# New places for attention blocks, state-space copies and state-space outputs between the projection units of a decoder block

## The chip, the core and the metric

The kernel runs on one core of a Trainium2 chip. Its engines are TensorE (PE, matrix multiplication; PEld is its loading of weights), VectorE (DVE), ScalarE (ACT) and GpSimd (POOL); SyncE (SP) issues the DMAs that bring weights and inputs from memory. Each engine works through its own queue in order and waits there for results of the others. The metric is the device time of one execution in microseconds (us), less is better.

## The reference

One decoder layer on 512 tokens of width 1024, in float32. A first RMSNorm is followed by one combined input projection; from it three branches are computed, gated, summed, projected and added to the input; a gated convolutional feed-forward layer and a last RMSNorm follow. Cut to what the change touches:

```python
proj = h @ w_in
qa, ka, va, qd, kd, vd, u, g = jnp.split(proj, cuts, axis=-1)
ya, _ = banded_attention(qa, ka, va, 127, attn_sinks)     # branch A: 8 heads, blocks of 128 queries
yb = dilated_attention(qd, kd, vd)                        # branch B: three dilations
yc = s5_mixer(u, ...)                                     # branch C: diagonal complex state space, 32 groups
gates = sigmoid(g)
merged = gates[0]*(ya @ w_branch_a) + gates[1]*(yb @ w_branch_b) + gates[2]*(yc @ w_branch_c)
x = x + merged @ w_out
x = x + conv_ffn(rmsnorm(x), w_up, conv_w, conv_b, w_down)
out = rmsnorm(x)
```

## The kernel before

Each large matrix product keeps float32 accuracy by splitting both operands into a high and a low part (`whi` and `wlo` for weights) and multiplying three times. A weight chunk comes by DMA into `raw`; ACT copies the high part out of it (L66, `whi<-raw`, 128x1024, two per chunk) and DVE subtracts to get the low part (L92, `wlo`).

The work is a list of **units**. A unit is one output tile of a large product: for a projection 24 matmuls of 128x512 (lines 171 to 173), after which ACT copies the result out of PSUM (`pj`, or `th` with a tanh for a gate). Unit 0 ends the projection of u; units 1 to 4 are the queries of branch A (qA), 5 its keys, 6 its values (vA), 7 to 14 the gates of A, 15 and 16 the keys of B, 17 and 18 queries of B, 19 and 20 the values of B (vB), 21 to 24 further queries of B, and from 25 on come the branch projections, gates, the output projection and the feed-forward. Two units share a chunk.

Small work is put between the units by hand. `before(u, f, ...)` has the functions f emitted ahead of unit u's matmuls. `run` emits, for each unit, the splits (whi, wlo) of the next chunk that are due, then the functions of `before`, then the unit; for units in the table `AUX_FIRST` the functions come ahead of those splits. So these tables set the order of every engine's queue. The pieces placed this way:

- `attn_a(i)`, block i of branch A, a generator of steps that `st_(A[i])` takes one at a time. Step 1: scores of half the heads (PE, `sc<-pj`) and their row maxima (DVE, `smA<-sc,maskA`). Step 2: the other half, then `esA` and eight exponentials (ACT), then the scaling by 1/l (DVE, L269). Then transposes (`pt<-ident,smA`) with copies `pTA` on ACT, the product with the values (`o<-pTA,VA`) and its copy `ya` (ACT, and `ya` again on DVE for the low part).
- branch C, in four parts j of 8 groups. `ssm_bd(j)` spreads a table and copies u into `us` (DVE, L624); `ssm_inj(j)` transposes (`pt<-ident,bd`), copies `inj` out (ACT) and fills `tz`; `ssm_cpow` computes the powers `Vw` on POOL with the scratch tiles `vt`; `ssm_ob(j)` copies from Vw into `ob` (ACT, four copies); `ssm_m1(j)` multiplies and scans in two steps (`z`, `X`); `ssm_m2(j)` is the output product (`o<-us,tz`, `o<-X,ob`), whose result goes in four copies of 32x512 to `yS`, two on ACT and two on DVE in turn (lines 724 to 729).
- `to_nat`, four transposes of the projected values (`pt<-ident,pj`, L737) and a copy on ACT (`VA`, `VB`).

Most intermediate tiles are taken by `slot()` from one pool `sl` of 46 equal buffers, in rotation: a new tile takes the buffer of the one taken 46 earlier, and its first writer waits until the last user of that one is done. PSUM has four kinds of banks (`mm`, `sc`, `pt`, `o`), two buffers each, in rotation as well.

Of the kernel before, what the change touches and what calls it, by code (L numbers as in the profile page):

```python
# [14 lines left out]
AX = mybir.AxisListType  # L15

NWARM = 32
AUX_FIRST = (7, 8, 10, 11, 14, 15, 18, 19, 20, 33, 35)
T = 512
DM = 1024  # L20
KD = DM // 128
# [10 lines left out]
def hybrid_block(  # L32
# [7 lines left out]
    V, S, G, PE, SY = nc.vector, nc.scalar, nc.gpsimd, nc.tensor, nc.sync  # L40
# [23 lines left out]
    def copy_act(o, i, scale=None):  # L64
        if scale is None:
            S.activation(o, i, AF.Copy)  # L66
        else:
            S.activation(o, i, AF.Copy, scale=scale)
# [128 lines left out]
    def before(u, *fns):  # L197
        plan.setdefault(u, []).extend(fns)

    def run(first, live):  # L200
# [31 lines left out]
        for u, (c, fn) in enumerate(units):  # L232
# [5 lines left out]
            later.clear()  # L238
            if u in AUX_FIRST:
                for f in fs:  # L240
# [372 lines left out]
    def expand(dst, src, j, scale=None):  # L613

        for g in range(2):
            p = slice(64 * g, 64 * g + 64)
            copy_act(dst[p, :, :, g, :], src[p].rearrange("p k (t j) h -> p t k j h", j=4)[:, :, :, j, :], scale=scale)

    def ssm_bd(j):
        for i in range(2):  # L620
            expand(BDs[j % 2][i], W[0][:, i], j)
        US[j] = slot([128, 4, 128], name="us")
        for tau in range(4):
            V.tensor_copy(US[j][32 * tau:32 * tau + 32],  # L624
                          uT[0][32 * j:32 * j + 32].rearrange("p t (c a) -> p t c a", a=4)[:, :, :, tau])

    def ssm_inj(j):
        bd = BDs[j % 2]
        INJ[j] = [slot([128, 4, 128], name="inj") for _ in range(2)]
        for i in range(2):  # L630
            pb = bank("pt")
            for t in range(4):
                PE.transpose(pb[:, t * 128:(t + 1) * 128],
                             bd[i][:, t].rearrange("p k g h -> p (k g h)"), ident)
            copy_act(INJ[j][i][:, :, :], pb[:, :].rearrange("p (t c) -> p t c", t=4))
        pk = bank("o", (128, 4, 32))
        for t in range(4):
            for i in range(2):
                PE.matmul(pk[:, t, :], bd[i][:, t].rearrange("p k g h -> p (k g h)"),
                          V0b[i][:, 4 * t + j].rearrange("p g h -> p (g h)"), start=(i == 0), stop=(i == 1))  # L640
        tz = TZ[j]
        for ti in range(4):
            for to in range(ti + 1, 4):
                b = 3 - (to - ti)
                copy_act(tz[32 * ti:32 * ti + 32, :, to, :], pk[32 * b:32 * b + 32, :, :])
        for ti in range(4):
            tt(tz[32 * ti:32 * ti + 32, :, ti, :], pk[96:128, :, :],
               DI[0][96:128].rearrange("p (t j) c -> p t j c", j=4)[:, :, j, :], ADD)

    def ssm_ob(j):  # L650
        for i in range(2):
            expand(OB[j][i], Vw[0][:, i], j, None if i == 0 else -1.0)
# [5 lines left out]
    def ssm_e(j):  # L658
        def v(tab):
            return tab.rearrange("p (t j) b -> p t j b", j=4)[:, :, j, :]  # L660

        b = [v(t)[:, :, None, :].to_broadcast([128, 4, 8, 16]) for t in eb]
        a = [v(t)[:, :, :, None].to_broadcast([128, 4, 8, 16]) for t in ea]
        E = [slot([128, 4, 8, 16], name="E") for _ in range(2)]
        t0 = slot([128, 4, 8, 16], name="et")
        tt(E[0], b[0], a[0], MUL, G)
        tt(t0, b[1], a[1], MUL, G)
        tt(E[0], E[0], t0, SUB, G)
        tt(E[1], b[0], a[1], MUL, G)
        tt(t0, b[1], a[0], MUL, G)  # L670
        tt(E[1], E[1], t0, ADD, G)
        Es[j] = [e[:, :, :, :].rearrange("p t a b -> p (t a b)") for e in E]
        A4s[j] = slot([128, 4, 128], name="a4")
        V.tensor_copy(A4s[j], mag4.rearrange("p (t j) -> p t j", j=4)[:, :, j:j + 1].to_broadcast([128, 4, 128]))
        V.memset(A4s[j][:, :, 0:1], 0.0)

    def ssm_m1(j):
        Er, Ei = Es.pop(j)
        s = []
        inj = INJ.pop(j)  # L680
        for i in range(2):
            pb = bank("sc", (128, 4, 128))
            for t in range(4):
                PE.matmul(pb[:, t, :], inj[i][:, t, :], US[j][:, t, :], start=True, stop=True)
            s.append(pb[:, :, :].rearrange("p t c -> p (t c)"))
        a, b, zr, zi = (slot([128, 512], name="z")[:, :] for _ in range(4))
        tt(zr, s[0], Er, MUL)
        tt(a, s[1], Ei, MUL)
        tt(zi, s[1], Er, MUL)
        tt(b, s[0], Ei, MUL)  # L690
        tt(zr, zr, a, ADD, G)
        tt(zi, zi, b, SUB, G)
        a4 = A4s.pop(j)[:, :, :].rearrange("p t c -> p (t c)")
        V.tensor_tensor_scan(a, a4, zr, 0.0, op0=MUL, op1=ADD)
        V.tensor_tensor_scan(b, a4, zi, 0.0, op0=MUL, op1=ADD)
        yield
        X = [slot([128, 4, 128], name="X") for _ in range(2)]
        x3 = slot([128, 512], name="xt")[:, :]

        def sh(v):  # L700
            return v.rearrange("p (t c) -> p t c", c=128)[:, :, 0:127]

        for i in range(2):
            G.memset(X[i][:, :, 0:1], 0.0)
        tt(zr, a, Er, MUL)
        tt(x3, b, Ei, MUL)
        tt(X[0][:, :, 1:128], sh(zr), sh(x3), SUB, G)
        tt(zi, a, Ei, MUL)
        tt(b, b, Er, MUL)
        tt(X[1][:, :, 1:128], sh(zi), sh(b), ADD, G)  # L710
        Xs[j] = X
        yield

    def ssm_m2(j):
        if not yS:
            yS.append(y8([128, 4, T], name="yS"))
        X, tz, us, ob = Xs.pop(j), TZ.pop(j), US.pop(j), OB.pop(j)
        py = bank("o", (128, 4, 128))
        for t in range(4):
            PE.matmul(py[:, t, :], tz[:, t].rearrange("p a b -> p (a b)"), us[:, t, :], start=True, stop=False)  # L720
            for i in range(2):
                PE.matmul(py[:, t, :], ob[i][:, t].rearrange("p k g h -> p (k g h)"), X[i][:, t, :],  # L722
                          start=False, stop=(i == 1))
        for tau in range(4):
            o = yS[0][32 * j:32 * j + 32].rearrange("p t (c a) -> p t c a", a=4)[:, :, :, tau]
            if tau % 2:
                V.tensor_copy(o, py[32 * tau:32 * tau + 32])
            else:
                copy_act(o, py[32 * tau:32 * tau + 32])


    def to_nat(src, name, strided=False):

        pb = bank("pt")
        v = src[:, :].rearrange("p (i r) -> p r i", r=4) if strided else src[:, :].rearrange("p (b i) -> p b i", b=4)
        for b in range(4):
            PE.transpose(pb[:, b * 128:(b + 1) * 128], v[:, b, :], ident)  # L737
        o = slot([128, 4, 128], name=name)
        copy_act(o, pb[:, :].rearrange("p (b c) -> p b c", b=4))
        return o  # L740

    proj = {}
# [10 lines left out]
    VA = []  # L753
# [89 lines left out]
    VB = {}  # L843
# [501 lines left out]
    def st_(g):  # L1345
        return lambda: next(g)

    CP = ssm_cpow()
    A = [attn_a(i) for i in range(4)]
    B = [attn_b(i) for i in range(2)]  # L1350
    M = [ssm_m1(j) for j in range(4)]
    before(0, lambda: pump(99), ssm_b, lambda: pump(6), ssm_phase)
# [2 lines left out]
    before(3, lambda: ssm_bd(0))  # L1355
    before(4, lambda: ssm_inj(0), lambda: ssm_bd(1), lambda: ssm_e(0), st_(CP))
    before(5, lambda: ssm_inj(1), lambda: ssm_bd(2))
    before(6, lambda: ssm_inj(2), lambda: ssm_bd(3), st_(CP))
    M = [ssm_m1(j) for j in range(4)]
    before(7, lambda: ssm_inj(3), st_(A[0]))  # L1360
    before(8, lambda: VA.append(to_nat(proj["vA"], "VA")), lambda: ssm_ob(0), st_(A[0]))
    before(9, st_(M[0]), lambda: ssm_ob(1))
    before(10, st_(A[0]), st_(M[0]), lambda: ssm_ob(2), st_(A[1]))
    before(11, st_(A[0]), lambda: ssm_ob(3), st_(A[1]))
    before(12, lambda: ssm_m2(0), lambda: ssm_e(1))
    before(13, st_(A[1]), st_(M[1]))
    before(14, st_(A[1]), st_(M[1]), st_(A[2]))
    before(15, st_(A[1]), lambda: ssm_m2(1), st_(A[2]))
    before(16, lambda: ssm_e(2))
    before(17, st_(A[2]), st_(M[2]))  # L1370
    before(18, st_(A[2]), st_(M[2]), st_(A[3]))
    before(19, st_(A[2]), lambda: ssm_m2(2), st_(A[3]))
    before(20, lambda: VB.setdefault(0, [to_nat(proj["vB", 0], "VB0")]), lambda: ssm_e(3))
    before(21, st_(A[3]), st_(M[3]), lambda: VB[0].append(to_nat(proj["vB", 0], "VB1", True)))
    before(22, st_(A[3]), st_(M[3]), lambda: VB.setdefault(1, [to_nat(proj["vB", 1], "VB0")]))
    before(23, st_(A[3]), lambda: VB[1].append(to_nat(proj["vB", 1], "VB1", True)))
# [44 lines left out]
```

## Time and profile before

| | |
|---|---|
| time, median of 3 runs | 839.66 us (839.02 to 839.73) |
| the profiled execution | 839.8 us, its span 838.0 us |
| PE busy | 815.6 us (97%) |
| DVE, ACT, POOL busy | 474.1 us (57%), 354.5 us (42%), 164.5 us (20%) |
| mean granted clock of TensorE | 0.991 of 2.4 GHz |

The span runs from the first to the last recorded instruction, and 1.8 us of the execution lie around it. PE is busy nearly throughout, so the questions are where it isn't, and where its clock is low; the places are found in the list of what PE waited for, and then on the timelines of the engines around them.

### The profile page before, as it was taken

The numbers are of one execution on the slowest core, as the hardware profiler recorded it, in microseconds if no ns is written. First come the engines' busy times: TensorE is split into PE (matmuls) and PEld (weight loads), VectorE is DVE, ScalarE is ACT, GpSimd is POOL, SyncE is SP. The second block draws the span as 40 slices with busy tenths as digits, with TensorE's granted clock in tenths as the row PEclk, the third lists the DMA queues.
The fourth block names the chain that finished last, engine by engine and source line by source line (L and its number), as shares of the span: only waits on it lengthen the run. The fifth ranks groups of instructions, "written<-read, shape, count | busy, mean of one in ns | idle before, by whom it ended". The sixth has DMA issues, their size and how long they took to land.

```text
span 838.0 us, 10521 instructions
## 1 busy us (share of the span) xinstructions
PE 815.6 (97%) x4085; PEld 675.9 (81%) x4085; DVE 474.1 (57%) x921; ACT 354.5 (42%) x665; POOL 164.5 (20%) x217
## 2 busy tenths in 40 slices
PE   8999899997999999999999999999999999999996
PEld 7978768775787888888878998888888888888885
DVE  7998387484645637263655456555655555422313
ACT  6446455434435555352444344444444443313212
POOL 6199652441200100023520000000000000002002
PEclk9999989998999999999999999999999999999999
DMA  9332031121322113232261313333233323412402
GB/s 241 102 104 97 1 100 52 51 79 46 78 68 90 52 51 102 79 101 72 101 236 65 101 52 101 101 101 100 101 101 100 102 76 101 153 61 89 151 0 101
DMA packets 68277, 76.60 MB, mean 91 GB/s; under 512 B 8160, under 2 KB 55556, under 8 KB 68228
## 3 DMA queue, kind: packets, MB, share of 16 engines
q1 hardware_dynamic: 67972, 75.89, 28.2%
q8 instruction: 32, 0.52, 0.3%
q0 software_dynamic: 256, 0.05, 0.1%
q14 instruction: 17, 0.14, 0.1%
HBM read 73.81 MB, written 2.12 MB: 91 GB/s over the span
## 4 chain that ended last, share of the span: by engine, by line
PE 80%; POOL 8%; DVE 6%; ACT 2%; issue 2%; DMA 2%; SPq 0%; POOLq 0%; DVEq 0%; ACTq 0%
PE up L171 10%; PE up L172 10%; PE up L173 10%; PE mm L171 9%; PE mm L173 9%; PE mm L172 9%; PE acc L178 6%; PE acc L179 6%; PE acc L177 6%; POOL esc L279 1%; POOL vt L279 1%; POOL t L279 1%; PE sc L898 1%; DMA raw<-in_w_in_dram 1%; PE o L722 1%
## 5 line engine op out<-in xcount | busy, mean ns | idle before, releaser
L92 DVE TENSOR_TENSOR wlo<-raw,whi 128x1024 fp32r<-128x1024 f32 (+1 forms) x126 | 150.0, 1200 | 136.0 <-ACT whi L66 135.8
L66 ACT ACTIVATE whi<-raw 128x1024 fp32r<-128x1024 f32 (+1 forms) x126 | 127.3, 1023 | 58.3 <-PE acc L179 56.2
L171 PE MATMUL up<-hTh,whi 128*128 128x512 f32 (+1 forms) x384 | 142.7, 372 | 0.0
L172 PE MATMUL up<-hTl,whi 128*128 128x512 f32 (+1 forms) x384 | 142.6, 371 | 0.0
L173 PE MATMUL up<-hTh,wlo 128*128 128x512 f32 (+1 forms) x384 | 142.6, 371 | 0.0
L171 PE MATMUL mm<-hTh,whi 128*128 128x512 f32 (+1 forms) x336 | 133.9, 399 | 2.7 <-ACT whi L66 2.7
L173 PE MATMUL mm<-hTh,wlo 128*128 128x512 f32 (+1 forms) x336 | 131.3, 391 | 1.6 <-DVE wlo L92 1.6
L172 PE MATMUL mm<-hTl,whi 128*128 128x512 f32 (+1 forms) x336 | 130.9, 390 | 0.0
L275 DVE SCALAR_TENSOR_TENSOR cc<-up,cpar,cc 128x511 f32<-128x511 f32 x88 | 65.9, 749 | 97.3 <-ACT cc L1110 95.7
L173 PEld LDWEIGHTS up<-hTh,wlo 128*128 128x128 f32 x384 | 72.4, 188 | 12.6
L171 PEld LDWEIGHTS up<-hTh,whi 128*128 128x128 f32 x384 | 72.4, 188 | 12.5
L172 PEld LDWEIGHTS up<-hTl,whi 128*128 128x128 f32 x384 | 72.4, 188 | 12.4
L171 PEld LDWEIGHTS mm<-hTh,whi 128*128 128x128 f32 x336 | 64.3, 191 | 17.9 <-ACT whi L66 3.1
L173 PEld LDWEIGHTS mm<-hTh,wlo 128*128 128x128 f32 x336 | 64.2, 191 | 15.2 <-DVE wlo L92 2.0
L172 PEld LDWEIGHTS mm<-hTl,whi 128*128 128x128 f32 x336 | 64.2, 191 | 11.9
L177 PE MATMUL acc<-whi,gh 128*128 128x512 f32 x172 | 66.9, 389 | 0.0
L178 PE MATMUL acc<-wlo,gh 128*128 128x512 f32 x172 | 66.9, 389 | 0.0
L179 PE MATMUL acc<-whi,gl 128*128 128x512 f32 x172 | 66.9, 389 | 0.0
L279 POOL TENSOR_TENSOR x<-x,gfin 128x512 f32<-128x512 f32 x4 | 5.2, 1289 | 296.8 <-ACT acc L1049 296.8
L1110 ACT ACTIVATE cc<-up,cpar 128x512 f32<-128x512 f32 x44 | 34.3, 779 | 61.2 <-PE up L173 60.4
L992 ACT ACTIVATE th<-mm 128x512 f32<-128x512 f32 x24 | 14.3, 594 | 75.2 <-PE mm L173 75.2
L66 ACT ACTIVATE gh<-cc 128x512 fp32r<-128x512 f32 x22 | 13.9, 632 | 59.4 <-DVE cc L279 59.4
(298 smaller groups left out, 1266.1 us busy)
## 6 DMA issues: line engine op xcount, KB each, us to landing
raw<-in_w_up_dram SPq DMA_DIRECT2D x22, 1024.0 KB, 5.1
raw<-in_w_in_dram SPq DMA_DIRECT2D x18, 1024.0 KB, 5.1
raw<-in_w_down_dram SPq DMA_DIRECT2D x10, 1024.0 KB, 5.0
x<-in_x_dram SPq DMA_DIRECT2D x8, 512.0 KB, 6.6
raw<-in_w_in_dram SPq DMA_DIRECT2D x8, 512.0 KB, 5.3
raw<-in_w_out_dram SPq DMA_DIRECT2D x4, 1024.0 KB, 5.1
raw<-in_w_branch_a_dram SPq DMA_DIRECT2D x4, 512.0 KB, 6.0
raw<-in_w_branch_c_dram SPq DMA_DIRECT2D x2, 1024.0 KB, 5.0
```

Of the source, the lines that this page charges most:

```text
L66: S.activation(o, i, AF.Copy)
L92: (lo_eng or V).tensor_tensor(view(lo), r, view(hi).bitcast(F32), op=ALU.subtract)
L171: PE.matmul(ps, wh, xh, start=first, stop=False)
L172: PE.matmul(ps, wh, xl, start=False, stop=False)
L173: PE.matmul(ps, wl, xh, start=False, stop=last)
L177: PE.matmul(ps, xh, wh, start=first, stop=False)
L178: PE.matmul(ps, xh, wl, start=False, stop=False)
L179: PE.matmul(ps, xl, wh, start=False, stop=last)
L275: emit(lambda: V.scalar_tensor_tensor(o, a, s, b, op0=op0, op1=op1))
L279: emit(lambda: (eng or V).tensor_tensor(o, a, b, op=op))
L992: S.activation(t, ps, AF.Tanh, scale=0.5)
L1110: S.activation(dst, ps, AF.Identity, bias=cpar[:, 3, f:f + 1], scale=cpar[:, 2, f:f + 1])
```

## The change

It moves steps among the units, takes five units (8, 10, 14, 18, 20) out of `AUX_FIRST`, and puts all four copies of each state-space output on ACT. A second, equal line that made the generators M anew is dropped; no step had been taken from the first ones.

```diff
-AUX_FIRST = (7, 8, 10, 11, 14, 15, 18, 19, 20, 33, 35)
+AUX_FIRST = (7, 11, 15, 19, 33, 35)
...
-            if tau % 2:
-                V.tensor_copy(o, py[32 * tau:32 * tau + 32])
-            else:
-                copy_act(o, py[32 * tau:32 * tau + 32])
+            copy_act(o, py[32 * tau:32 * tau + 32])
...
-    before(6, lambda: ssm_inj(2), lambda: ssm_bd(3), st_(CP))
-    before(7, lambda: ssm_inj(3), st_(A[0]))
-    before(8, lambda: VA.append(to_nat(proj["vA"], "VA")), lambda: ssm_ob(0), st_(A[0]))
-    before(9, st_(M[0]), lambda: ssm_ob(1))
-    before(10, st_(A[0]), st_(M[0]), lambda: ssm_ob(2), st_(A[1]))
-    before(11, st_(A[0]), lambda: ssm_ob(3), st_(A[1]))
+    before(6, lambda: ssm_inj(2), lambda: ssm_bd(3), st_(CP), st_(A[0]))
+    before(7, st_(A[0]), lambda: ssm_inj(3))
+    before(8, lambda: VA.append(to_nat(proj["vA"], "VA")), lambda: ssm_ob(0), lambda: ssm_ob(1))
+    before(9, st_(A[0]), st_(M[0]), lambda: ssm_ob(2))
+    before(10, lambda: ssm_ob(3), st_(A[0]), st_(M[0]), st_(A[1]))
+    before(11, st_(A[1]))
...
-    before(15, st_(A[1]), lambda: ssm_m2(1), st_(A[2]))
-    before(16, lambda: ssm_e(2))
+    before(15, st_(A[1]), st_(A[2]))
+    before(16, lambda: ssm_m2(1), lambda: ssm_e(2))
...
-    before(19, st_(A[2]), lambda: ssm_m2(2), st_(A[3]))
-    before(20, lambda: VB.setdefault(0, [to_nat(proj["vB", 0], "VB0")]), lambda: ssm_e(3))
+    before(19, st_(A[2]), st_(A[3]))
+    before(20, lambda: ssm_m2(2), lambda: VB.setdefault(0, [to_nat(proj["vB", 0], "VB0")]), lambda: ssm_e(3))
```

Three places in the engines' queues show what that moves.

The first is ACT from the copy of unit 6 on, with the engines whose semaphores each instruction waits for (the 49 belongs to the semaphore's name). Before, the two `inj` copies of the last state-space part come first and the exponentials of block 0 after the first `ob`:

```order
L66 ACTIVATE pj<-mm 128x512 [waits PE_49,Pool_49]
L66 ACTIVATE inj<-pt 128x512 [waits PE_49] x2
L66 ACTIVATE tz<-o 32x4x32 [waits PE_49]
L66 ACTIVATE tz<-o 32x4x32 x5
L66 ACTIVATE whi<-raw 128x1024 [waits DMAHW4_49,DVE_49]
L992 ACTIVATE th<-mm 128x512 [waits PE_49,Pool_49]
L66 ACTIVATE VA<-pt 128x512 [waits PE_49,Pool_49]
L66 ACTIVATE ob<-Vw 64x16x16 x2
L68 ACTIVATE ob<-Vw 64x16x16 x2
L780 ACTIVATE esA_1233<-esA_1233 128x8 [waits DVE_49]
L782 ACTIVATE smA,lA_1232<-smA,nmA_1231 128x128 x2
```

And now:

```order
L66 ACTIVATE pj<-mm 128x512 [waits PE_49]
L777 ACTIVATE esA_1173<-esA_1173 128x8 [waits DVE_49]
L779 ACTIVATE smA,lA_1172<-smA,nmA_1171 128x128 [waits Pool_49]
L779 ACTIVATE smA,lA_1172<-smA,nmA_1171 128x128
L779 ACTIVATE smA,lA_1172<-smA,nmA_1171 128x128 [waits Pool_49]
L779 ACTIVATE smA,lA_1172<-smA,nmA_1171 128x128 x3
L779 ACTIVATE smA,lA_1172<-smA,nmA_1171 128x128 [waits Pool_49]
L779 ACTIVATE smA,lA_1172<-smA,nmA_1171 128x128
L66 ACTIVATE inj<-pt 128x512 [waits PE_49,Pool_49] x2
L66 ACTIVATE tz<-o 32x4x32 [waits PE_49]
L66 ACTIVATE tz<-o 32x4x32 x5
L66 ACTIVATE whi<-raw 128x1024 [waits DMAHW4_49]
```

The exponentials of block 0 stand ahead of the last `inj` copies, and through the rotation of the buffers it is now these two copies that wait for POOL: they take the buffers of the two scratch tiles `vt`, which `th` and `VA` took before. Both splits (`whi`) of the next chunk stand behind them.

The second is DVE at units 8 to 11, from the scaling of block 0 to the first row maximum of block 1. Before:

```order
L269 TENSOR_SCALAR smA<-smA,lA_1232 128x128 x8
L92 TENSOR_TENSOR wlo<-raw,whi 128x1024 x2
L279 TENSOR_TENSOR z<-sc,E 128x512 x4
L694 SCALAR_TENSOR_TENSOR z<-a_992,z 128x512
L695 SCALAR_TENSOR_TENSOR z<-a_992,z 128x512
L279 TENSOR_TENSOR z<-z,E 128x512
L279 TENSOR_TENSOR xt<-z,E 128x512
L279 TENSOR_TENSOR z<-z,E 128x512 x2
```

And now:

```order
L269 TENSOR_SCALAR smA<-smA,lA_1172 128x128 x8
L279 TENSOR_TENSOR tz<-o,DI 32x4x32 x4
L92 TENSOR_TENSOR wlo<-raw,whi 128x1024 x3
L279 TENSOR_TENSOR z<-sc,E 128x512 x4
L694 SCALAR_TENSOR_TENSOR z<-a_992,z 128x512
L695 SCALAR_TENSOR_TENSOR z<-a_992,z 128x512
L92 TENSOR_TENSOR wlo<-raw,whi 128x1024
L279 TENSOR_TENSOR ya_1363<-o,ya_1362 128x4x128
L279 TENSOR_TENSOR z<-z,E 128x512
L279 TENSOR_TENSOR xt<-z,E 128x512
L279 TENSOR_TENSOR z<-z,E 128x512 x2
```

The maxima of block 1 have one more split (`wlo`) and the second part of `ya` ahead of them, behind the scans.

The third is ACT at units 18 to 20, from the `ya` copy of block 2 to the copies around the first `VB`. Before:

```order
L66 ACTIVATE ya_1411<-o 128x4x128
L66 ACTIVATE yS<-o 32x512 x2
L780 ACTIVATE esA_1999<-esA_1999 128x8
L782 ACTIVATE smA,lA_1998<-smA,nmA_1997 128x256 x8
L66 ACTIVATE whi<-raw 128x1024
L66 ACTIVATE pj<-mm 128x512
L66 ACTIVATE VB_2135<-pt 128x512
L66 ACTIVATE whi<-raw 128x1024
```

And now:

```order
L66 ACTIVATE ya_1362<-o 128x4x128
L777 ACTIVATE esA_2005<-esA_2005 128x8
L779 ACTIVATE smA,lA_2004<-smA,nmA_2003 128x256 x8
L66 ACTIVATE whi<-raw 128x1024
L66 ACTIVATE pj<-mm 128x512
L66 ACTIVATE whi<-raw 128x1024
L66 ACTIVATE yS<-o 32x512 x4
L66 ACTIVATE VB_2142<-pt 128x512
L66 ACTIVATE pj<-mm 128x512
```

The `yS` copies of state-space part 2 stood ahead of the exponentials of block 3, and now stand behind them and behind the copy `pj` of unit 19, four in a row.

## Rows read from the trace of the kernel before

**Rows 1.** Busy time of each engine over the span, first part of the page.

```profile
PE 815.6 (97%) x4085; PEld 675.9 (81%) x4085; DVE 474.1 (57%) x921; ACT 354.5 (42%) x665; POOL 164.5 (20%) x217
```

**Rows 2.** What PE waited for: total us, times, longest us.

```profile
PE pt L737 <- ACT pj L66: 5.4, 1, 5.4
PE mm L171 <- ACT whi L66: 2.7, 1, 2.7
PE mm L173 <- DVE wlo L92: 1.6, 1, 1.6
```

**Rows 3.** Stretches: length, busy us (count) per engine, granted clock, DMA, GB/s.

```profile
107.10:112.80 5.70, 5.70 (x18) 4.51 (x18) 5.43 (x6) 1.50 (x4) 2.52 (x2) 0.55 0.56 184
...
201.80:207.80 6.00, 5.99 (x16) 4.88 (x17) 3.81 (x9) 1.55 (x2) 0.00 (x0) 0.50 0.07 8
```

**Rows 4.** Timeline of ACT: start us, us, instruction [idle before <-releaser].

```profile
97.62 0.60 ACT L992 ACTIVATE th<-mm 128x512 f32<-128x512 f32 x1 [10.30 <-PE mm L173]
...
98.80 0.83 ACT L66 ACTIVATE ob<-Vw 64x256 f32<-64x256 f32 x2
...
100.50 0.21 ACT L780 ACTIVATE esA<-esA 128x8 f32<-128x8 f32 x1
...
103.69 1.04 ACT L66 ACTIVATE whi<-raw 128x1024 fp32r<-128x1024 f32 x1
```

**Rows 5.** Timeline of POOL, 80 to 99 us.

```profile
80.80 3.95 POOL L279 TENSOR_TENSOR vt<-V,t 128x256 f32<-128x256 f32 x4
...
86.09 2.36 POOL L279 TENSOR_TENSOR vt<-Vw,t 128x256 f32<-128x256 f32 x4
88.42 2.44 POOL L279 TENSOR_TENSOR Vw<-vt 128x256 f32<-128x256 f32 x2
...
96.85 1.42 POOL L279 TENSOR_TENSOR Vw<-vt 128x256 f32<-128x256 f32 x2
```

**Rows 6.** Timeline of PE, 76 to 122 us.

```profile
76.24 0.48 PE L171 MATMUL mm<-hTh,whi 128*128 128x512 f32 x1
...
81.78 1.04 PE L633 MATMUL pt<-ident,bd 128*128 128x128 f32 x8
...
84.46 0.72 PE L766 MATMUL sc<-pj 64*128 64x128 f32 x8
...
90.66 0.60 PE L737 MATMUL pt<-ident,pj 128*128 128x128 f32 x4
...
121.65 0.50 PE L171 MATMUL mm<-hTh,whi 128*128 128x512 f32 x1
```

**Rows 7.** Timeline of DVE, 79 to 118 us.

```profile
79.82 4.45 DVE L624 COPY us<-uT 32x512 f32<-32x512 f32 x4
...
87.50 0.29 DVE L773 CUSTOM_DVE_ANT_0 smA<-sc,maskA 128x128 f32<-128x128 f32 x1
...
114.17 0.66 DVE L279 TENSOR_TENSOR z<-z,E 128x512 f32<-128x512 f32 x1
...
117.65 0.41 DVE L773 CUSTOM_DVE_ANT_0 smA<-sc,maskA 128x256 f32<-128x256 f32 x1
```

**Rows 8.** Timeline of PE, 186 to 211 us.

```profile
186.78 0.49 PE L720 MATMUL o<-us,tz 128*128 128x128 f32 x2
...
189.66 1.13 PE L766 MATMUL sc<-pj 64*128 64x256 f32 x8
...
210.59 1.03 PE L796 MATMUL pt<-ident,smA 128*128 128x128 f32 x8
```

**Rows 9.** Timeline of ACT, 191 to 202 us.

```profile
191.99 1.06 ACT L66 ACTIVATE yS<-o 32x512 f32<-32x512 f32 x1 [1.14 <-DVE yS L727]
196.06 0.21 ACT L780 ACTIVATE esA<-esA 128x8 f32<-128x8 f32 x1 [3.01 <-DVE esA L279]
...
201.16 0.60 ACT L66 ACTIVATE pj<-mm 128x512 f32<-128x512 f32 x1
```

**Rows 10.** Timeline of DVE, 193 us.

```profile
193.08 1.06 DVE L727 COPY yS<-o 32x512 f32<-32x512 f32 x1 [1.13 <-ACT yS L66]
```

More of the change, by code (lines that the diff above doesn't have):

```diff
@@ L1357, in hybrid_block @@
     before(5, lambda: ssm_inj(1), lambda: ssm_bd(2))
-    before(6, lambda: ssm_inj(2), lambda: ssm_bd(3), st_(CP))
-    M = [ssm_m1(j) for j in range(4)]
-    before(7, lambda: ssm_inj(3), st_(A[0]))
-    before(8, lambda: VA.append(to_nat(proj["vA"], "VA")), lambda: ssm_ob(0), st_(A[0]))
-    before(9, st_(M[0]), lambda: ssm_ob(1))
-    before(10, st_(A[0]), st_(M[0]), lambda: ssm_ob(2), st_(A[1]))
-    before(11, st_(A[0]), lambda: ssm_ob(3), st_(A[1]))
+    before(6, lambda: ssm_inj(2), lambda: ssm_bd(3), st_(CP), st_(A[0]))
[4 more added lines that the diff above has]
+    before(11, st_(A[1]))
     before(12, lambda: ssm_m2(0), lambda: ssm_e(1))
```

## The prediction

> **What bounds the kernel now.** I read the busy shares first: PE is busy 815.6 of 838.0 us [rows 1], so only PE's waits and the stretches in which it runs at less than full clock can give much. The list of PE's waits is second, and it has only three long ones in the part of the program that the change touches [rows 2]: 2.7 us for a `whi`, 1.6 for the `wlo` of the same chunk, and 5.4 before line 737 for a `pj`. Third, the stretches behind these waits: after the two on the weights the granted clock is 0.55 of 2.4 GHz from 107.1 to 112.8 us, after the third it is 0.50 from 201.8 to 207.8 [rows 3], that is about the lower level, 1.2 GHz. So each place costs its wait and then the slow unit behind it. Last come the timelines of the engines that PE waits for at the two places [rows 4 to 10].
>
> At full clock a unit takes 5.54 us of PE (unit 6, 76.24 to 81.78), and a state-space input step (transposes and `o<-V0b,bd`) 2.68 (81.78 to 84.46) [rows 6].
>
> **Units 18 to 20: gained.** Call T the start of the second half of block 3's scores, 189.66 [rows 8]. Before, these scores stand behind `m2(2)`, which is 2.88 of PE (186.78 to 189.66). Its four outputs alternate between ACT and DVE, 1.06 each, each idle beforehand for the other [rows 9, 10]. So DVE is done with the last copy only at 193.08 + 1.06 = 194.14, T + 4.5. The remaining row maxima of block 3 wait behind it, `esA` starts at 196.06 = T + 6.4, the eight exponentials and two splits follow, and the `pj` of unit 19 ends at 201.16 + 0.60 = 201.76, T + 12.1 [rows 9]. PE has done scores (1.13) and unit 19 (5.54) at T + 6.7. The difference is the wait of 5.4 [rows 2].
>
> Now `m2(2)` and its four copies stand behind unit 19. The maxima can start when the first scores are written, about T + 1.45 instead of T + 4.5. All that follows on ACT moves by 3.0: `esA` T + 3.4, `pj` done T + 9.1. PE gets to the four transposes at T + 6.7 + 2.88 = T + 9.5. So the wait is gone, with 0.4 to spare. With it goes the slow stretch: transposes and unit 20 took 210.59 - 201.8 = 8.8 [rows 8], where at full clock they take 0.5 (the 0.60 of line 737 [rows 6], less what runs beside the next unit) + 5.54, so 2.75 are lost to the clock. `m2(2)` itself is moved, not added. Gain: 5.4 + 2.75 = **8.15**. Four yS copies in a row on ACT cost 4 x 1.06 = 4.2, about what the alternation took (four of 1.06, one behind another): next to nothing, since in it either engine only waited for the other. If ACT had no room there, it would be on the path (a rival below).
>
> **Units 6 to 11: lost.** I replay the queues from unit 6.
>
> Block 0's first scores now come ahead of unit 6, 0.6 to 0.7 of PE [rows 6], so unit 6 runs from 76.9 to 82.4. Their maxima stand on DVE behind the four `us` copies, which end at 79.82 + 4.45 = 84.27 [rows 7]; the second scores need their banks, so PE waits to about 85.1, the maxima at 0.29 each [rows 7]. Second scores 0.7 and input step 2.68 end at 88.5, unit 7 at 94.0.
>
> ACT has meanwhile done block 0's exponentials (3.2, as from 100.50 to 103.69 [rows 4]) and comes to the last two `inj` copies. In the new order these wait for POOL as well: they take buffers of the two `vt`. POOL's chain has pairs of `vt` and `Vw` there, and the first of the last pair of `Vw` starts at 96.85 and ends about 0.75 later, at 97.6 [rows 5]. In the profile before, `th` took that buffer and started at 97.62 after 10.30 us of idle time [rows 4]. The view puts that down to a matmul of line 173, but a unit that ended at 90.66 [rows 6] can't hold it until then; POOL's end, to the hundredth, does. `th` and `VA` had time there. `inj` has not: the transposes of vA ahead of unit 8 need a `pt` bank that the `inj` copy gives back. I make it 97.6 + 0.6 = 98.2, a wait of **4.2** on PE from 94.0.
>
> That is a wait between the 4.3 (2.7 + 1.6) and the 5.4 behind which the clock fell [rows 2, 3]; I let the transposes and unit 8 run like transposes and unit 20, 8.8. They end at 107.0. The transposes of block 0 (1.0, as [rows 8]) and the first scan products (sixteen matmuls, a bit less than twice the 1.04 of eight [rows 6]: 1.9) lead to 109.9, unit 9 to 115.4. Its weights aren't late any more: their `whi` stand behind `inj` and `tz`, some 5 us ahead of need. So the 4.3 and the slow stretch of before are saved here, and are paid at unit 8 instead.
>
> A new wait comes at unit 11. Block 1's second scores need its first maxima, and these stand on DVE behind the scans and behind the second part of `ya`, whose copy on ACT stands behind `whi` and `ob`. From unit 9's end: `th` 0.60, `whi` 1.04, four `ob` 1.7 (98.80 to 100.50), `ya` 0.6, all by [rows 4]; on DVE `ya` 0.7 (estimate, as the 0.66 of a `z` of the same size), the rest of the scans 3.5 (114.17 to 117.65), maxima 1.4 (at 0.41 less overlap) [rows 7]. Sum 9.5, to 124.9; half of the scores' 1.13 [rows 8] comes after the last maximum: unit 11 starts at 125.5. PE alone would be there at 115.4 + 1.0 (product with the values, estimate as the transposes) + 1.1 + 5.54 = 123.0, so it waits 1.9 after its scores. Before, unit 11 started at 121.65 [rows 6]. Loss: **3.85**.
>
> Bounds of this loss. If PE's clock stays up at unit 8 (wait of 4.2 with no slow unit), PE is 2.75 sooner, unit 11 starts at 122.75 to 123.1, and the loss is 1.1 to 1.4. If the wait at unit 11 too is followed by a slow unit, it is 3.85 + 2.75 = 6.6. POOL's end is the other unknown. A group of four `vt` takes 3.95 beside the `us` copies and 2.36 without [rows 5]; block 0's scalings now fall beside the chain, which could bring up to 1.6 more. A pair of `Vw` takes 2.44 where it met a `wlo` of DVE, else 1.42 [rows 5]; where it doesn't meet one now, 1.0 less. I take 0, since the copies on DVE stay where the chain is slowest.
>
> The Trainium skill, "GPSIMD Engine Reference", section 8 "Key points", speaks against the change here: GpSimd shares its SBUF interfaces with VectorE, in contention with DVE instructions in a 2-port mode or with two SBUF inputs. The rows on `vt` and `Vw` agree (3.95 against 2.36); by it the scalings that move beside the chain make POOL later, and the sum would be 837.1.
>
> Behind unit 21 the order stays but for who copies `yS`, at units where ACT idles for 3 us and more ([rows 4, 9] show idle times of 10.30 and 3.01): nothing. The dropped line costs nothing.
>
> **Sum.** The profiled execution took 839.8, 838.0 of it span and 1.8 around it; the median of the runs is 839.66, 0.14 lower. 839.8 + 3.85 - 8.15 = **835.5**.
>
> **Rivals.**
> 1. The clock stays up at unit 8. For it: after 2.7 alone the matmuls ahead of the 1.6 wait still ran at full rate. Against: behind the two together and behind 5.4 it fell [rows 2, 3], and 4.2 is next to those. 839.8 + 1.4 - 8.15 = 833.1. Chance 0.20.
> 2. POOL's chain ends at another time: 1.6 later gives 835.5 + 1.6 = 837.1, 1.0 sooner 834.5. For it: the spread of [rows 5]. Against: most of the chain keeps its company on DVE. 0.12.
> 3. The wait ahead of unit 20 goes only in part: the maxima are held by something other than the copies, `pj` stays at T + 12.1, and PE waits 12.1 - 9.5 = 2.6 with the slow stretch kept at 2.75. Only 5.4 - 2.6 = 2.8 is gained: 839.8 + 3.85 - 2.8 = 840.85, no change. Against: the idle of 3.01 before `esA` is put down to DVE [rows 9]. 0.07.
> 4. Slower: the four copies on ACT stand on PE's path at each of the four outputs. Each puts two more copies of 1.06 ahead of what PE needs next, 2.1, four times 8.5: 835.5 + 8.5 = 844.0. It decides if ACT has less than 2.1 idle before its next copy for PE. Against: the idle times named above. 0.05.
> 5. Further slow stretches: the wait at unit 11 slows its unit too, 835.5 + 2.75 = 838.25. For: the clock did fall at each long wait. Against: 1.9 is below all that were followed by it. 0.08, half of which I put beyond 838.0 into no change.
>
> **How the numbers follow.** The forecast has the remaining 0.48. Its own steps carry some 1.6 us of error (the end of POOL's chain, the maxima). The first rival sets the low end, 833.1 less 0.9 for smaller waits at unit 11: 832.2. The high end takes in the late POOL chain and the slow stretch at unit 11: 838.6. Left out are rivals 3 and 4 and tails, under 0.2. No change means within 0.2%, 1.7 us, which is what a measurement here can tell, 838.0 to 841.3: rival 3 and half of 5, with tails, 0.13. Slower is rival 4 and mishaps of both places, 0.06. Faster has 0.81.
>
> **What would show it.** In the profile after: no wait of PE ahead of line 737 near 200 us, and the clock at 1.0 through unit 20; `esA` of block 3 about 3.4 after its scores start. No wait of PE for `whi` or `wlo` near 105 us, but one of some 4 us ahead of the transposes of unit 8, with ACT idle before `inj` until POOL's `Vw`, and a granted clock near 0.5 through unit 8; a wait of about 2 ahead of unit 11 for row maxima. I am wrong if `inj` starts well before POOL's `Vw`, if unit 8 runs at full clock, or if unit 20 still starts behind a wait.

## The result and the profile after

The changed kernel takes 832.35 us (median of 4 runs, 831.74 to 834.41), the kernel before 839.69 beside it. The ratio over all runs of both, with its 95% interval, is 0.9918 (0.9900 to 0.9937). The forecast was 835.5, its range 832.2 to 838.6. The profiled execution took 834.41, the longest of the four, against 839.8 of the one before: 5.4 less.

What PE waited for in the changed kernel (total us, times, longest us):

```profile
PE sc L763 <- DVE mxA L770: 3.4, 2, 2.3
```

The three waits of [rows 2] are gone, and two waits for row maxima have come. The stretches that matter (columns as in [rows 3]):

```profile
60.00:64.00 4.00, 4.00 (x14) 3.31 (x14) 2.89 (x7) 3.66 (x12) 4.00 (x10) 0.60 0.30 88
...
88.00:94.00 6.00, 6.00 (x29) 5.75 (x28) 2.30 (x11) 3.29 (x17) 6.00 (x10) 0.50 0.00 0
...
107.00:113.00 6.00, 6.00 (x40) 5.41 (x39) 3.94 (x6) 4.17 (x8) 1.55 (x2) 1.00 0.25 87
...
200.00:206.00 6.00, 6.00 (x32) 4.99 (x31) 3.32 (x7) 5.63 (x7) 0.00 (x0) 1.00 0.24 60
```

107 to 113 us and 200 to 206 us, slow before [rows 3], run at full clock. Slow instead are 88 to 94 us, at 0.50, and 60 to 64 us, in work that the change doesn't touch; the profile before doesn't have the latter, and it is in three of the ten experiments' profiles (e3, e7, e8) but not in the others. It comes and goes between executions and costs this one some 1.7 us.

PE around the two places, after:

```profile
75.54 1.04 PE L633 MATMUL pt<-ident,bd 128*128 128x128 f32 x8
...
86.89 1.64 PE L763 MATMUL sc<-pj 64*128 64x128 f32 x8 [2.25 <-DVE mxA L770]
...
100.87 0.60 PE L734 MATMUL pt<-ident,pj 128*128 128x128 f32 x4
...
106.78 1.04 PE L793 MATMUL pt<-ident,smA 128*128 128x128 f32 x8
...
123.95 1.82 PE L763 MATMUL sc<-pj 64*128 64x256 f32 x8 [1.13 <-DVE mxA L770]
...
131.27 0.38 PE L720 MATMUL o<-us,tz 128*128 128x128 f32 x2
...
180.39 1.08 PE L799 MATMUL o<-pTA,VA 128*64 128x512 f32 x4
...
190.16 1.14 PE L763 MATMUL sc<-pj 64*128 64x256 f32 x8
...
199.49 0.63 PE L734 MATMUL pt<-ident,pj 128*128 128x128 f32 x4
...
205.44 1.04 PE L793 MATMUL pt<-ident,smA 128*128 128x128 f32 x8
```

And the same works' starts before that [rows 6, 8] don't hold:

```profile
73.66 1.04 PE L633 MATMUL pt<-ident,bd 128*128 128x128 f32 x8
...
127.25 0.38 PE L720 MATMUL o<-us,tz 128*128 128x128 f32 x2
...
177.01 1.08 PE L802 MATMUL o<-pTA,VA 128*64 128x512 f32 x4
```

Set against each other: the transposes of input step 2 start at 75.54 instead of 73.66 (+1.9, of it 0.2 from the first 57 us and 1.7 from the clock at 60 us); the first `m2` at 131.27 instead of 127.25 (so units 6 to 11 lose 4.0 - 1.9 = **2.1**); the product with the values ahead of unit 18 at 180.39 instead of 177.01 (0.6 gained on the way, 0.5 of it at one set of transposes of block 2, which take 1.03 where they took 1.51); the transposes ahead of unit 21 at 205.44 instead of 210.59 (so units 18 to 20 gain 3.4 + 5.15 = **8.5**). Sum 1.9 + 2.1 - 0.6 - 8.5 - 0.3 (from there to the end) = -5.4.

Who held PE, on ACT, DVE and POOL of the changed kernel (start, length):

```profile
96.62 1.29 ACT L66 ACTIVATE inj<-pt 128x512 f32<-128x512 f32 x2 [2.80 <-POOL Vw L279]
...
193.84 0.21 ACT L777 ACTIVATE esA<-esA 128x8 f32<-128x8 f32 x1 [2.94 <-DVE esA L279]
...
198.84 0.57 ACT L66 ACTIVATE pj<-mm 128x512 f32<-128x512 f32 x1
```

```profile
82.33 3.98 DVE L624 COPY us<-uT 32x512 f32<-32x512 f32 x4
86.33 0.29 DVE L770 CUSTOM_DVE_ANT_0 smA<-sc,maskA 128x128 f32<-128x128 f32 x1
...
94.46 3.50 DVE L269 TENSOR_SCALAR smA<-smA,lA 128x128 f32<-128x128 f32 x8
...
123.13 0.41 DVE L770 CUSTOM_DVE_ANT_0 smA<-sc,maskA 128x256 f32<-128x256 f32 x1
```

```profile
93.54 2.36 POOL L279 TENSOR_TENSOR vt<-Vw,t 128x256 f32<-128x256 f32 x4
95.86 1.43 POOL L279 TENSOR_TENSOR Vw<-vt 128x256 f32<-128x256 f32 x2
```

At unit 7 the maxima (86.33) stand behind the four `us` copies, as forecast, and PE waits 2.25 us. But the clock falls right there, so the second scores take 1.64 instead of 0.72, and PE reaches the transposes of unit 8 only at 100.87. The `inj` copies did wait for POOL's `Vw`, until 96.62, but that was over by then: the wait of 4.2 that was forecast has no time left in which to show. Unit 8 runs at full clock (100.87 to 106.78). At unit 11 the maxima of block 1 start at 123.13 behind the scans, as forecast, and PE waits 1.13 for them, with scores of 1.82. At unit 20 `esA` starts 3.7 after the scores (190.16) and `pj` ends at 199.4, just as PE arrives (199.49): no wait. The four `yS` copies start at 200.39 and take 4.34 in a row, and nobody waits for them.

### The profile page after: what moved, and what is told of

The parts are those of the page before. It is cut to its first block, busy times and chain, and to the rows that moved or that the text cites. A ratio compares the mean times of both kernels' runs of the same rounds, so it can differ in the third digit from the quotient of the medians.

```text
span 832.6 us, 10517 instructions
## 1 busy us (share of the span) xinstructions
PE 815.8 (98%) x4085; PEld 677.2 (81%) x4085; DVE 470.8 (57%) x913; ACT 363.3 (44%) x673; POOL 160.1 (19%) x217
## 3 DMA queue, kind: packets, MB, share of 16 engines
HBM read 73.81 MB, written 2.12 MB: 91 GB/s over the span
## 4 chain that ended last, share of the span: by engine, by line
PE 84%; DVE 8%; DMA 2%; ACT 2%; issue 1%; POOL 1%; SPq 1%; POOLq 0%; DVEq 0%; ACTq 0%
PE mm L171 10%; PE up L172 10%; PE up L171 10%; PE up L173 10%; PE mm L172 9%; PE mm L173 9%; PE acc L178 6%; PE acc L179 6%; PE acc L177 6%; DVE wlo L92 1%; DVE us L624 1%; PE sc L895 1%; PE sc L763 1%; PE sc L684 1%; PE o L722 1%
```

## Experiments

In every one the kernel before ran beside it, on the same chip.

**The two places apart.** e1 has the old places in units 6 to 11, e2 has new places only there.

```diff
 e1, against the changed kernel
-AUX_FIRST = (7, 11, 15, 19, 33, 35)
+AUX_FIRST = (7, 8, 10, 11, 15, 19, 33, 35)
-    before(6, ...) to before(11, ...) of the changed kernel
+    before(6, ...) to before(11, ...) of the kernel before
 e2, against the changed kernel
-    before(15, ...) to before(20, ...) of the changed kernel, copies on ACT
+    before(15, ...) to before(20, ...) of the kernel before, alternating copies, 14, 18, 20 in AUX_FIRST
```

> The changed kernel with the places of units 6 to 11 as they were before (and units 8 and 10 back in AUX_FIRST); the places of units 12 to 20 and the state-space copies on ACT as changed. Theory (the two stretches are independent; the changed kernel's profile against the one before gives +2.1 us up to unit 12 and -8.5 us between units 17 and 21): 839.7 - 8.5 = 831.2 us, 1.1 faster than the changed kernel's 832.35, with PE's waits for whi and wlo near 103 us back and no wait ahead of unit 20. Rival (the new places of units 6 to 11 pay too, or the gain at unit 20 needs them): 834 us or more.

> The changed kernel with only the places of units 6 to 11 changed; units 12 to 20, AUX_FIRST for them and the alternating state-space copies as before. Theory: it loses 2.1 us against before, 841.8 us (840.5 to 843), with a wait of PE for the row maxima ahead of unit 7's second scores (2.3 us), the clock near 0.5 for some 10 us behind it, no wait for whi or wlo near 105 us, and the 5.4 us ahead of unit 20 kept. Rival (the new places gain because the waits for the weights are gone): 838 us or less.

e1: 830.16, ratio 0.9898 (0.9884 to 0.9913). e2: 840.85, ratio 1.0028 (1.0018 to 1.0037). The product of the two ratios is 0.9926, the changed kernel's is 0.9918: within the error the places add, and of the two one gains 1.0% and the other loses 0.3%. e1 is 1.0 us better than expected, e2 lies in its expected range. In e2's profile, though, the loss has another form than in the profile above:

```profile
84.68 1.13 PE L766 MATMUL sc<-pj 64*128 64x128 f32 x8 [1.98 <-DVE mxA L773]
...
97.04 0.66 PE L737 MATMUL pt<-ident,pj 128*128 128x128 f32 x4 [2.94 <-ACT inj L66]
...
104.60 1.04 PE L796 MATMUL pt<-ident,smA 128*128 128x128 f32 x8
```

```profile
97.00:100.00 3.00, 2.96 (x10) 2.47 (x11) 0.59 (x2) 2.82 (x8) 0.04 (x1) 0.59 0.00 0
```

The wait for the maxima (1.98, above it was 2.25) is not followed by a slow clock here: the granted clock is 1.00 from 84 to 96 us. So PE is at unit 8 in time to meet the late `inj`, waits 2.94, and then the clock falls, 0.59 from 97 to 100 us. This is the course that the forecast described. The expectation of a slow clock behind the first wait was wrong: nearly the same wait is followed by it in one profile and not in the other.

**The copies.** e3 lets them alternate again.

```diff
-            copy_act(o, py[32 * tau:32 * tau + 32])
+            if tau % 2:
+                V.tensor_copy(o, py[32 * tau:32 * tau + 32])
+            else:
+                copy_act(o, py[32 * tau:32 * tau + 32])
```

> The changed kernel with one edit undone: the four state-space output copies alternate between ACT and DVE again. Theory (the order of the steps does it, and the copies only wait for each other): no change against the changed kernel, 832.4 us within 0.7. Rival (copies on one engine free DVE for the maxima and the wlo): 2 to 8 us slower, 834.5 to 840.

832.63, ratio 0.9923 (0.9908 to 0.9938): no change against 0.9918, within some 0.2%. In the new places the engine that copies doesn't matter.

Up to unit 12 e3 has the places of the changed kernel, and its profile shows a third course of units 6 to 11. PE:

```profile
87.08 1.13 PE L766 MATMUL sc<-pj 64*128 64x128 f32 x8 [1.88 <-DVE mxA L773]
...
96.36 0.66 PE L737 MATMUL pt<-ident,pj 128*128 128x128 f32 x4
```

The slow stretch at 60 us has made PE 2.5 late here (the transposes of input step 2 start at 76.16 instead of 73.66). It waits 1.88 for the maxima with no slow clock behind, and comes to unit 8 when the first of the two `inj` copies, which start at 95.70 behind POOL's `Vw`, is just done: no wait, and unit 8 at full clock. From the transposes of input step 2 to the first `m2` this execution takes 51.4 us, where the kernel before takes 53.6, e2 55.5 and the changed kernel 55.7. So the loss of units 6 to 11 isn't a fixed price of the new places: it depends on when PE comes there, and on the clock. One profile per kernel doesn't tell how often each course is taken; that e2 loses 0.28% is the mean of ten runs.

**The step ahead of block 3's scores.** e9 puts `ssm_m2(2)` back ahead of them; e10 does that with alternating copies.

```diff
-    before(19, st_(A[2]), st_(A[3]))
-    before(20, lambda: ssm_m2(2), lambda: VB.setdefault(...), lambda: ssm_e(3))
+    before(19, st_(A[2]), lambda: ssm_m2(2), st_(A[3]))
+    before(20, lambda: VB.setdefault(...), lambda: ssm_e(3))
```

> The changed kernel with one step back: the output step of state-space part 2 stands again ahead of block 3's second scores (unit 19); its four copies stay on ACT. T is the start of these scores. Theory (the place of the step decides, through what stands ahead of the maxima on DVE and of the exponentials on ACT): the maxima no longer wait, since DVE has no copies, but the exponentials stand behind four copies on ACT and start at T + 4.5 instead of T + 3.4; pj is done at T + 10.2, PE is ready at T + 6.7 and waits 3.4 us ahead of unit 20: 832.4 + 3.4 = 835.8 us, 838.5 where the clock falls behind the wait. Rival (copies on one engine are enough, the place doesn't matter): 832.4.

> The kernel of e9 with the copies alternating between ACT and DVE as well. Theory: the maxima wait for DVE's second copy, the exponentials start at T + 6.4, PE waits 5.4 us ahead of unit 20 and unit 20 is slow: 832.4 + 8.2 = 840.6 us. Rival (the alternation costs nothing here either, as in e3): the same as e9.

e9: 838.52, ratio 0.9995 (0.9983 to 1.0006). e10: 840.98, ratio 1.0030 (1.0019 to 1.0041). First PE and ACT in e9, then PE, ACT and DVE in e10:

```profile
191.22 1.13 PE L763 MATMUL sc<-pj 64*128 64x256 f32 x8
...
201.46 1.12 PE L734 MATMUL pt<-ident,pj 128*128 128x128 f32 x4 [3.44 <-ACT pj L66]
```

```profile
191.33 4.36 ACT L66 ACTIVATE yS<-o 32x512 f32<-32x512 f32 x4 [2.24 <-PE o L722]
195.70 0.21 ACT L777 ACTIVATE esA<-esA 128x8 f32<-128x8 f32 x1
```

```profile
191.16 1.13 PE L766 MATMUL sc<-pj 64*128 64x256 f32 x8
...
203.31 1.12 PE L737 MATMUL pt<-ident,pj 128*128 128x128 f32 x4 [5.36 <-ACT pj L66]
```

```profile
197.55 0.21 ACT L780 ACTIVATE esA<-esA 128x8 f32<-128x8 f32 x1 [3.00 <-DVE esA L279]
```

```profile
194.57 1.06 DVE L727 COPY yS<-o 32x512 f32<-32x512 f32 x1 [1.13 <-ACT yS L66]
```

The waits are 3.44 and 5.36, to the tenth those expected, and `esA` starts at T + 4.48 and T + 6.39 (T is 191.22 and 191.16). In e9 the four copies on ACT stand ahead of `esA`; in e10 DVE's second copy (194.57) stands ahead of the maxima. The time of e9 is at the end of its expectation where the clock falls behind the wait. By the ratios e9 is 0.0077 or 6.5 us behind the changed kernel, and e10 0.0112 or 9.4: the place of this one step carries the gain of units 18 to 20, and in the old place the copies' engine does matter (e10 is 0.0035 behind e9).

**What holds units 6 to 11.** e4 takes the `us` copies out of the maxima's way; e5 also keeps `inj` off the buffers of `vt`.

```diff
 e4
-    before(6, lambda: ssm_inj(2), lambda: ssm_bd(3), st_(CP), st_(A[0]))
+    before(6, lambda: ssm_inj(2), st_(A[0]), lambda: ssm_bd(3), st_(CP))
 e5, with the edit of e4
     def ssm_inj(j):
         bd = BDs[j % 2]
+        if j == 3:
+            for _ in range(2):
+                held.append(slot([128, 4, 128], name="held"))
+                G.memset(held[-1][:, 0:1, 0:1], 0.0)
+    before(10, lambda: [G.memset(t[:, 0:1, 0:1], 0.0) for t in held])
```

> The changed kernel with one step moved ahead of unit 6: block 0's first scores and maxima come before the spreading of the last table and its four us copies, so the maxima don't stand behind these on DVE. Theory (this wait and the slow clock behind it are what units 6 to 11 lose): no wait ahead of the second scores, unit 7 at full clock, PE at the transposes ahead of unit 8 about 7 us sooner; there it now meets the inj copies that wait for POOL until about 97 us and waits some 3.5 us. If the clock stays up behind that wait: 828.7; if it falls, unit 8 is slow instead of unit 7 and little is gained: 831.4. Rival (the maxima are not what holds PE there): 832.4, unchanged, with the wait still there.

> The kernel of e4 with one more edit: two empty tiles take the buffers of the two vt ahead of the last inj and are kept until unit 10, so that no early tile gets these buffers. Theory (the 5.4 us that PE waits ahead of unit 8 in e4, and the slow unit behind it, come from inj getting vt's buffers and so waiting for POOL's last Vw): inj starts right behind the exponentials, near 89.5 instead of 96.6 us; no wait at the transposes of unit 8, unit 8 at full clock; 5.4 + 2.4 = 7.8 us less than e4's 833.0: 825.2 (824.5 to 827). Rival (inj waits for POOL or PE for something else too, such as Vw or the copies ob that come later): 830 or more, with a wait of PE near unit 8 or 9.

e4: 832.99, ratio 0.9930 (0.9914 to 0.9947), no change within the error, and beyond the 831.4 that I expected even with the slow unit. Its profile, PE, ACT and POOL:

```profile
97.27 1.11 PE L734 MATMUL pt<-ident,pj 128*128 128x128 f32 x4 [5.41 <-ACT inj L66]
...
105.61 1.03 PE L793 MATMUL pt<-ident,smA 128*128 128x128 f32 x8
```

```profile
96.62 1.28 ACT L66 ACTIVATE inj<-pt 128x512 f32<-128x512 f32 x2 [7.05 <-POOL Vw L279]
```

```profile
80.82 4.02 POOL L279 TENSOR_TENSOR vt<-V,t 128x256 f32<-128x256 f32 x4
...
88.50 1.42 POOL L279 TENSOR_TENSOR Vw<-vt 128x256 f32<-128x256 f32 x2
```

The wait for the maxima is gone, and PE waits 5.41 for `inj` instead, with transposes and unit 8 in 8.34 behind it. The idle time of 7.05 ahead of `inj` is put down to POOL's `Vw`. Whatever PE saves ahead of unit 8, it gives back there, since POOL's chain doesn't end sooner.

e5: 828.97, ratio 0.9874 (0.9853 to 0.9895), by the ratios 0.0056 or 4.7 us better than e4, and not 7.8. ACT, PE and POOL:

```profile
89.82 1.06 ACT L66 ACTIVATE inj<-pt 128x512 f32<-128x512 f32 x2
...
97.05 0.85 ACT L66 ACTIVATE ob<-Vw 64x256 f32<-64x256 f32 x2 [1.32 <-POOL Vw L279]
```

```profile
91.89 0.60 PE L738 MATMUL pt<-ident,pj 128*128 128x128 f32 x4
...
97.82 1.04 PE L797 MATMUL pt<-ident,smA 128*128 128x128 f32 x8
...
116.32 2.49 PE L767 MATMUL sc<-pj 64*128 64x256 f32 x8 [2.45 <-DVE mxA L774]
```

```profile
96.29 2.40 POOL L279 TENSOR_TENSOR Vw<-vt 128x256 f32<-128x256 f32 x2
```

`inj` starts at 89.82 right behind the exponentials, and unit 8 runs without a wait at full clock, 91.89 to 97.82, as expected. The rest of the expectation failed: the `ob` copies wait for `Vw`, the first until 97.05 and the next until this last pair (2.40) is done, the next `whi` (at 101.93) stands behind them, and with it the `wlo`, the scan and the maxima of block 1, so that the wait at unit 11 grew from 1.11 (e4) to 2.45 and the clock falls behind it. So POOL's end is felt by another way: no longer through the buffers of `inj`, but through the data of `ob`.

**Both ways closed, from the better half.** e6, e7 and e8 start from e1. Its waits for the weights come from ACT, where `th` and `VA` hold the buffers of `vt`, and `ob` needs `Vw`, both ahead of the exponentials and `whi`.

```diff
 e7 (e6 has this as well)
-    before(8, lambda: VA.append(to_nat(proj["vA"], "VA")), lambda: ssm_ob(0), st_(A[0]))
-    before(9, st_(M[0]), lambda: ssm_ob(1))
-    before(10, st_(A[0]), st_(M[0]), lambda: ssm_ob(2), st_(A[1]))
-    before(11, st_(A[0]), lambda: ssm_ob(3), st_(A[1]))
-    before(12, lambda: ssm_m2(0), lambda: ssm_e(1))
+    before(8, lambda: VA.append(to_nat(proj["vA"], "VA")), st_(A[0]))
+    before(9, st_(M[0]), lambda: ssm_ob(0))
+    before(10, st_(A[0]), st_(M[0]), lambda: ssm_ob(1), st_(A[1]))
+    before(11, st_(A[0]), lambda: ssm_ob(2), st_(A[1]))
+    before(12, lambda: ssm_ob(3), lambda: ssm_m2(0), lambda: ssm_e(1))
 e8 (e6 has this as well); hold() takes the two empty tiles of e5,
 which are written once more at unit 10, as there
-    before(7, lambda: ssm_inj(3), st_(A[0]))
+    before(7, lambda: ssm_inj(3), st_(A[0]), hold)
```

> The kernel of e1 (old places in units 6 to 11, new ones from 12 on) with two edits: empty tiles take the two vt's buffers ahead of th and VA of units 7 and 8, and each group of ob copies comes one unit later. Theory (whi of unit 9 is late because th waits for POOL through its buffer and then ob for Vw, both ahead of it on ACT): th near 91 us, the exponentials near 94, whi near 97; no wait of PE between units 6 and 12 and no slow unit: 830.2 - 4.3 - 2.8 = 823 us (822 to 825). Rival (another step is late there, such as the copies pTA or ya behind the ob, or the DMA of the weights): 826 or more, with a wait that names it.

> The kernel of e1 with only the ob copies one unit later; th and VA still take vt's buffers. Theory: th still starts near 97.7 us and the exponentials follow VA at once, so whi of unit 9 is 1.7 us sooner (102.2): the waits of 2.7 and 1.6 shrink to 2.6 in all or less, 828.5 us; 826 if the clock stays up behind them. Rival (th doesn't wait for POOL, ob alone is what holds ACT): th near 91 us, no waits left, 823, as e6.

> The kernel of e1 with only the buffers edit of e6; ob stays ahead of the exponentials. Theory: th near 91 us, but ob waits for the last Vw until about 98.2, and whi of unit 9 is at most 0.8 us sooner than 103.9: 829.4 us. Rival (the buffer of th alone holds ACT): the waits go, 823.

e6: **823.72**, ratio 0.9828 (0.9802 to 0.9854). e7: 827.17, 0.9859 (0.9843 to 0.9875). e8: 828.08, 0.9870 (0.9854 to 0.9887). ACT in e6, e7 and e8:

```profile
90.31 0.60 ACT L989 ACTIVATE th<-mm 128x512 f32<-128x512 f32 x1 [3.65 <-PE mm L173]
...
96.51 1.05 ACT L66 ACTIVATE whi<-raw 128x1024 fp32r<-128x1024 f32 x1
```

```profile
97.74 0.60 ACT L989 ACTIVATE th<-mm 128x512 f32<-128x512 f32 x1 [8.46 <-POOL Vw L279]
...
102.11 1.06 ACT L66 ACTIVATE whi<-raw 128x1024 fp32r<-128x1024 f32 x1
```

```profile
97.68 0.85 ACT L66 ACTIVATE ob<-Vw 64x256 f32<-64x256 f32 x2 [2.12 <-POOL Vw L279]
...
102.60 1.05 ACT L66 ACTIVATE whi<-raw 128x1024 fp32r<-128x1024 f32 x1
```

In e7 `th` still waits for `Vw` (8.46 us of idle time), in e8 `ob` does (2.12), and `whi` comes at 102.1 and 102.6. Only with both edits is it early, at 96.51, and then PE has no single wait above 0.8 us past its start, and the mean granted clock of this execution is 0.999. By these rows the two rivals of e7 and e8, that one of the two alone holds ACT, are out. The times say it less sharply. Both kernels came out 1.3 us better than expected. Their profiled executions had the slow stretch at 60 us, and of the 4.5 and 5.4 us that they took longer than e6's, 2.6 and 4.2 lie ahead of the edited units. Since PE comes that much later against POOL, e7's profile has only one wait for the weights left (0.98, for a `wlo`) and e8's none. Whether this holds for all of their runs isn't shown, and e6's slowest run (826.72) is close to e7's fastest (826.87). By the ratios e6 is 0.0090 or 7.6 us faster than the changed kernel, and 1.7% faster than the kernel before.

## Why the prediction was right, and where it was not

**Units 18 to 20.** Right in mechanism and size: 8.15 forecast, 8.5 measured, and e1, which has the new places only from unit 12 on, gains 0.0102 or 8.6 us (with the small pieces of units 12 to 17 in it). The wait of 5.4 went, and transposes and unit 20 took 5.95 (199.49 to 205.44) instead of 8.8, 2.8 less. The step `esA` at T + 3.4 came out at T + 3.7 and PE arrived with 0.1 to spare instead of 0.4. e9 and e10 show each part of the chain by itself.

**yS copies at no cost.** Right (e3); rival 4 is out.

**Units 6 to 11.** A loss, as forecast, but in the profiled execution of 2.1 instead of 3.85; e2 as a whole is 0.28% slower than before, 2.3 us. Of the three terms two were off.
- The maxima behind the `us` copies: PE's resumption was forecast at 85.1, and is 86.89, with the shift of 1.9 in it: right. What it starts was not: I priced no slow clock behind this wait, and in the profiled execution it fell there and cost 5.1 us (86.89 to 100.87 is 14.0, where 0.7 + 2.7 + 5.5 = 8.9 were forecast).
- The wait of 4.2 for `inj` and the slow unit 8: in the profiled execution both are absent, because PE is late; in e2 they are there as 2.94 and 7.6 instead of 4.2 and 8.8. The copy starts at 96.62 (in e2 at 96.39) and not at 97.6. In e4, where POOL's chain starts as before (80.82 against 80.80 [rows 5]), the pair of `Vw` at 88.50 takes 1.42 where it took 2.44: its collision with a `wlo` is gone, which is the -1.0 of rival 2, given too little. In the changed kernel's own profile that pair is as short, but other groups are longer (a `Vw` pair of 2.20 at 83.64, a `vt` group of 2.74 at 85.80), and the copy is early because the chain began at 79.94.
- The wait at unit 11: 9.5 forecast from unit 9's end to the last maximum and measured 115.0 to 124.6, 9.6; right. PE loses 1.13 in the wait and 0.7 in scores drawn out by the maxima, 1.8 together; 1.9 was forecast.

So the step that doesn't hold in general is the one that lets PE come to unit 8 at 94.0 and wait there. In e2, e9 and e10 PE comes at 94.1 to 94.4 and waits 2.9 to 3.0. In the changed kernel's profile, slow from unit 7 on, and in e3's, late since 60 us, it comes later and doesn't wait. What PE loses ahead of unit 8 it doesn't wait at unit 8, since POOL's end doesn't come later when PE does: the last pair of `Vw` starts at 95.86 in the changed kernel and at 94.92 in e3, where PE is late, and at 95.63 in e2 and 95.87 in e4, where it isn't.

For the profiled execution the account is 835.5 + 1.9 at its start - 1.7 too much in units 6 to 11 - 0.4 too little at unit 20 - 0.9 in small pieces that no term had = 834.4. The median is 3.15 below the forecast. The three faster executions have no profile, so it isn't shown which course they took; were they without the 1.9, that would explain most of the 2.1 between the median and the profiled execution. The median lies 0.15 above the lower edge of the range, which rival 1 had set and not a term that was off: that it fell within is in part luck.

**The rule on POOL and DVE.** The scalings moved beside POOL's chain, and POOL didn't become later: the last `vt` group takes 2.36 beside them and `Vw` 1.43. The Trainium skill, "GPSIMD Engine Reference", section 8, names two-input DVE instructions and 2-port modes as what contends. The rows agree with the rule for a two-input `wlo`: beside it a `Vw` pair takes 2.40 in e5, as the 2.44 of [rows 5]. For the scalings the 837.1 that was worked out was wrong: they cost POOL nothing. That they have one tensor as input doesn't explain it, since the `us` copies have one too, and beside them a group of four `vt` out of `Vw` takes 3.53 in e3 instead of 2.36. Why the copies slow POOL and the scalings don't stays open.

**A correction.** The kernel's description says that a new tile takes the buffer taken 46 earlier. That is too simple, I think: long-lived tiles are skipped, and a new tile gets the buffer whose last use comes first in the program. No run here shows that rule. For `vt` the successors named there are the real ones, as e5, e6 and e7 show.

## What to carry to other kernels

A wait that moves from one engine to another is not gone: look for the instruction with a fixed end (here POOL's last `Vw`) and for every queue through which it is felt, by data (`ob`) and by buffers (`th`, `inj`), and move all of them; with one of the two ways closed, e7 and e8 gained about half of what e6 did. An output copy that nobody waits for should stand behind the work that the next large product needs, whichever engine does it. Price a wait of PE of the size seen here (2 us and more) with and without the slow clock behind it, and don't add two such prices that lie close together.

## What the runs showed of the hardware

The clock after a wait isn't a matter of the wait alone. For the maxima at unit 7 PE waited 2.25 us in the changed kernel and 1.98 in e2; the clock fell to 0.50 in the one and stayed at 1.00 in the other. After the 1.88 of e3 it stayed up as well. After 2.45 (e5), 2.94 (e2), 3.44 (e9) and 5.4 it fell. But it also fell at 60 us, behind waits of 0.8 and 0.2, in the changed kernel's profile and not in the one before, which has the same waits (0.79 and 0.22).

DVE pays for POOL too. The eight scalings of block 0 take 1.66 with POOL idle (before), 3.50 beside POOL's chain (after) and 4.62 in e4, where POOL keeps its pace; here the rows of before and of e4:

```profile
104.26 1.66 DVE L269 TENSOR_SCALAR smA<-smA,lA 128x128 f32<-128x128 f32 x8
```

```profile
90.21 4.62 DVE L269 TENSOR_SCALAR smA<-smA,lA 128x128 f32<-128x128 f32 x8
```
